# Down-projection weight sums: two by accumulating DMA transfers instead of VectorE adds, and another load order of the quarters

## The chip, the cores and the metric

The kernel runs on one core of a Trainium2 chip. That core has a matrix engine (TensorE, "PE" in the profile, with its weight loads as "PEld"), VectorE (DVE), ScalarE (ACT), GpSimd (POOL) and SyncE (SP). Each engine works through its own queue of instructions in order and waits on semaphores. SP and POOL also issue DMA transfers, which run on 16 shared DMA engines: SP the plain loads from device memory, POOL those that add the source to what is in the destination. The metric is the device time of one launch in microseconds, as the median of several runs; the profile is of one further execution.

## What is computed

A trunk of two layers, run on 512 tokens of one request and 256 of another. Each layer is a half-weighted SwiGLU feed-forward block (FFN), a token mixer, and another FFN, so there are four FFNs (f0 to f3 in the kernel). The change is in the down projection (`w2`) of the FFNs.

```python
def swiglu_ffn(x, w1, w2):
    gate, up = jnp.split(x @ w1, 2, axis=-1)
    return (jax.nn.silu(gate) * up) @ w2

for li in range(DEPTH):
    x = x + 0.5 * swiglu_ffn(rmsnorm(x, norm_g[li, 0]), ffn_w1[li, 0], ffn_w2[li, 0])
    ...
    x = x + mix
    x = x + 0.5 * swiglu_ffn(rmsnorm(x, norm_g[li, 2]), ffn_w1[li, 1], ffn_w2[li, 1])
return rmsnorm(x, final_norm_g)
```

D_MODEL is 1024, D_FF is 2816, all inputs are float32.

## The kernel before

**Precision.** Every float32 weight or activation is split into a high part (a cast on ScalarE) and a low part (a subtraction of the cast from the original on VectorE, for some weights on GpSimd), and each product takes three matmuls: high by high, high by low, low by high.

**Seven products.** The large matrix products are blocked two by two and done with seven block products instead of eight, so sums of weight blocks are needed. For the down projection, a group covers four blocks of 128 rows of `w2`, cut into four quarters of 128 x 1024 numbers: a11, a12 (the left 512 columns, in `srcs` 0 and 1) and a21, a22 (the right 512 columns, in `srcs` 2 and 3). The operands of the seven products are

- p1: a11, p2: a12, p4: a22, as they are loaded;
- p5: a21 + a22, made in place in a21 by a transfer (`into`, L160) that GpSimd issues;
- p7 (`s3`): a21 + a11, made in two half tiles of their own, into which the quarter a21 is loaded once more (L222) and a11 is added by a transfer (L223);
- p6: a11 + (a21 + a22), the "second" sum, made in place in a11;
- p3: a12 + that, the "fourth" sum, made in place in a12.

The second and fourth sums of a down group are VectorE adds (L245), one ahead of p6's split and one ahead of p3's, held in program order (`pin`). The up projection (`w1`) has its own groups of seven, called pairs here, of half the size; they have the same two sums on VectorE, behind the splits of p5 and p4.

**Order of work.** An FFN has five groups. Each is four columns of the up projection (product order p1, p7, p2, p5, p4, p6, p3; matmuls at L669, 384 columns each, 12 to a product) and then one down group. A full group (`DOWN`: p1, p2, p5, p4, p7, p6, p3) has its matmuls at L778, 512 columns each, 18 to a product; after each product's accumulation VectorE adds the PSUM banks into the residual x (L841). An FFN's last group (`LAST`: p1, p2, p6, p7, p4, p5, p3) has 27 matmuls to a product (L811), because two left-over row blocks, the "tail", ride along; the tail has quarters of its own, whose second and fourth sums are already transfers, issued behind the splits of the tail's p1 and p2.

**Staging.** Raw quarters are loaded on SP's queue (L175) into four raw buffers (`wr`, `RAWBUFS`), used in rotation; a down group takes all four, an up pair two. A load waits until the last reader of what its buffer held is done. `stage_next` runs one step of the next group: cast (L238) and subtraction (L239) of one operand into split buffers (`w`, eight of them, `WBUFS`). `ahead` stages as many steps as there are free split buffers, each time PE has finished with a product. So splits run several products ahead of their use. The tail's splits are at L383 and L384. The group after the current one may have its raw loads issued once at most four steps of a down group are left (`inuse`). The instructions' order within each queue is set by a scheduler that goes by its own cost model and by the order of the program; instructions in `pin` keep the program's order.

In an up pair ScalarE copies the result of p1 out of its PSUM bank (L686) and that of p7 (L691), before PE adds p2 and p4 into the same banks; it also does the gates (L694, L709). VectorE's sums of the pair's results are L697 to L710.

Of the kernel before, what the change touches and what calls it, by code (L numbers as in the profile page):

```python
# [58 lines left out]
class Trunk:  # L59
# [102 lines left out]
    def load_next(self):  # L162
        key, srcs, shape, how = self.queue.pop(0)
        if how in (TOK, OUT):
            self.loaded.append((self.tok_steps(key, srcs, how), lambda left: 4 if left > 4 else 0))
            return
        raws = []
        for src in srcs:
            t = self.wp.tile([P, 1024], F32, tag="wr", name=self.name("wr"), bufs=RAWBUFS)
            raw = t[:, : shape[0] * shape[1]].rearrange("p (a b) -> p a b", a=shape[0])  # L170
            if len(srcs) < 4:
                src = src.rearrange("(k p) c -> p k c", p=P)
            step = shape[0] // 2 if key in EARLY else shape[0]
            for lo in range(0, shape[0], step):
                self.last_load = self.nc.sync.dma_start(raw[:, lo : lo + step], src[:, lo : lo + step])  # L175
            raws.append(raw)
        if len(raws) == 1:
            steps = self.plain_steps(key, raws[0], shape)
        else:
            steps = self.quad_steps(key, raws, srcs, how)  # L180
        n, more = len(raws), self.more.get(key)
        if more:
            tail = self.tail_steps(key, more, how)
            steps = [step for both in zip(steps, tail) for step in both]
        if n == 4:
            inuse = lambda left: 4 if left > (8 if more else 4) else 0
        else:
            inuse = lambda left: n
        self.loaded.append((steps, inuse))
# [17 lines left out]
    def quad_steps(self, key, raws, srcs, order):  # L207
        nc = self.nc
        flat = lambda t: t.rearrange("p a b -> p (a b)")
        up = len(raws) == 2  # L210
        if up:
            a11, a12, a21, a22 = (flat(t[:, h : h + 4, :]) for t in raws for h in (0, 4))
            part = lambda i, k: srcs[i].rearrange("(k p) c -> p k c", p=P)[:, k : k + 4, :]
            three = [part(1, 0)] + ([part(0, 4)] if order == OPEN else [])
        else:
            a11, a12, a21, a22 = (flat(t) for t in raws)
            three = [srcs[2][:, i : i + 1, :] for i in range(2)]
        spare = up and (PLAIN[key[0]] == 2 or key[1] > 3)
        s3 = []
        for i, src in enumerate(three):  # L220
            t = self.wp.tile([P, 512], F32, tag="s3", name=self.name("s3"), bufs=2)
            self.last_load = nc.sync.dma_start(t.rearrange("p (a b) -> p a b", a=src.shape[1]), src)  # L222
            self.into(t, a11 if up else a11[:, i * 512 : (i + 1) * 512])  # L223
            s3.append(t)
        self.into(a21, a22)
        if order == OPEN:
            self.into(s3[1], a21)

        def split(name, srcs, eng=None):
            if up:  # L230
                w = self.wtile()
                hi, lo = w[:, :512], w[:, 512:]
            else:
                hi, lo = self.wtile(), self.wtile()
            n = srcs[0].shape[-1]
            for i, src in enumerate(srcs):
                h, l = (t[:, i * n : (i + 1) * n] for t in (hi, lo))
                nc.scalar.copy(h, src)  # L238
                (eng or nc.vector).tensor_sub(l, src, h.bitcast(F32))  # L239
            view = lambda t: t.rearrange("p (a b) -> p a b", a=4 if up else 2)  # L240
            self.staged[(*key, name)] = (view(hi), view(lo), 1 if up else 2)

        own = {"p1": [a11], "p2": [a12], "p3": [a12], "p4": [a22], "p5": [a21], "p6": [a11], "p7": s3}
        pin = self.tc.keep_in_program_order
        add = {"second": lambda: nc.vector.tensor_add(a11, a11, a21), "fourth": lambda: nc.vector.tensor_add(a12, a12, a11)}  # L245
        before = {} if up else {"p6": "second", "p3": "fourth"}
        behind = {"p5": "second", "p4": "fourth"} if up else {}

        if order == OPEN:
            own.update({"p3": s3[1:], "p7": s3[:1]})  # L250
            add = {"second": lambda: self.into(a11, a21)}
            behind, pin = {"p1": "second"}, lambda ins: None

        def step(name):
            if name in before:
                pin(add[before[name]]())
            split(name, own[name], nc.gpsimd if spare and name == "p5" else None)
            if name in behind:
                pin(add[behind[name]]())

        gated = lambda i: order == OPEN and i >= GATED
        return [(1 if up else 2, lambda name=name: step(name), gated(i)) for i, name in enumerate(order)]

    def tail_steps(self, key, srcs, order):
# [368 lines left out]
    def gated(self, pss, act=None, dve=None):  # L633
        t = self.tmp(H)
        with self.tc.issue_after(act) if act else nullcontext():
            self.nc.scalar.activation(t, pss[0], AF.Silu)
        with self.tc.issue_after(dve) if dve else nullcontext():
            self.nc.vector.tensor_mul(t, t, pss[1])
        return t
# [1183 lines left out]
```

## Time and profile before

| what | value |
|---|---|
| median of 3 runs | 2753.04 us (2751.81 to 2754.34) |
| profiled execution, its own time | 2752.44 us |
| its span, first to last instruction | 2750.7 us |
| granted TensorE clock, mean | 0.999 |
| ScalarE waiting for the second or fourth sum on VectorE | 175.9 us in 52 waits, up to 6.1 |
| ScalarE waiting for a transfer into a raw buffer | 66.4 us in 28 waits, up to 5.2 |
| DMA moved | 340.71 MB, 124 GB/s on the mean |
| of it on GpSimd's queue | 97.41 MB, 20.4% of the 16 DMA engines |

How to read the rows. A row of a timeline has the start in us from the span's start, the duration (of several merged instructions from the first start to the last end), engine, source line, operation, output<-input by the program's names, and the count; in brackets the idle time of the engine before it and what ended that. A row of the waits has who waited, for whom, the total in us, how often, and the longest. A group row has the count, the busy time in us and the mean of one in ns, then the idle time before. A row of DMA issues has the count, the size of one and the median time from issue to landing in us. "SPq" is SP's queue of DMA issues; a row of it shows the issue, not the landing.

### The profile page before, as it was taken

The page shows a single profiled execution, that of the slowest core. Times are in us where ns is not written, and L with a number is a line of the kernel's source. Part 1 is how long each engine was busy: PE and PEld are TensorE (multiplying, and loading weights), DVE is VectorE, ACT ScalarE, POOL GpSimd, SP SyncE. Part 2 cuts the span into 40 slices and gives each one's busy share as a digit, 9 for nine tenths or more (in the row PEclk, how much of TensorE's full clock was granted, in tenths as well). Part 3 has the DMA queues.
Part 4 walks back from the last instruction along what each step waited for, and adds up shares of the span by engine and source line. Part 5 has one row for each costly group of instructions (what it writes and reads, how often), then busy time and mean ns, then how long its engine had stood idle before and what let it go on. Part 6 is the DMA issues. An engine that isn't in the chain of part 4 may idle for free.

```text
span 2750.7 us, 41100 instructions
## 1 busy us (share of the span) xinstructions
PE 2732.9 (99%) x15059; PEld 2540.4 (92%) x15059; DVE 2192.8 (80%) x3791; ACT 1408.3 (51%) x2665; POOL 470.4 (17%) x534
## 2 busy tenths in 40 slices
PE   9999999999999999999999999999999999999998
PEld 8999999989999889999998999999888889999997
DVE  8788788767877888788878987887847869788877
ACT  6344444634455675444455643444458855444454
POOL 1111121200000111211121121112005621211120
PEclk9999999999999999999999999999999999999999
DMA  6554556741122755655455555545424435555453
GB/s 178 127 128 116 125 142 165 226 142 39 39 59 65 201 131 124 146 134 127 118 132 141 116 146 130 130 114 141 129 78 111 89 75 121 143 134 131 117 133 111
DMA packets 363259, 340.71 MB, mean 124 GB/s; under 512 B 15320, under 2 KB 275888, under 8 KB 363056
## 3 DMA queue, kind: packets, MB, share of 16 engines
q1 hardware_dynamic: 307200, 227.18, 27.9%
q0 software_dynamic: 51552, 97.41, 20.4%
q10 hardware_dynamic: 4304, 13.49, 1.4%
q8 instruction: 118, 1.93, 0.3%
q14 instruction: 85, 0.70, 0.1%
HBM read 228.45 MB, written 15.73 MB: 89 GB/s over the span
## 4 chain that ended last, share of the span: by engine, by line
PE 80%; DVE 1%; ACT 1%; DMA 0%; issue 0%; POOL 0%; ACTq 0%; POOLq 0%; DVEq 0%
PE ps L669 33%; PE ps L778 12%; PE ps L994 6%; PE ps L811 6%; PE ps L379 5%; PE ps L378 5%; PE ps L380 5%; PE ps L1057 3%; PE ps L1162 1%; PE ps L475 1%; PE ps L1677 1%; PE ps L1138 1%; PE ps L1639 0%; PE ps L1640 0%; PE ps L1689 0%; PE ps L1690 0%
## 5 line engine op out<-in xcount | busy, mean ns | idle before, releaser
L669 PE MATMUL ps<-big,w 128*128 128x384 f32 x6972 | 1213.2, 334 | 0.0
L669 PEld LDWEIGHTS ps<-big,w 128*128 128x128 f32 x6972 | 1209.5, 188 | 1.4
L238 ACT CAST w<-wr 128x512 fp32r<-128x512 f32 (+1 forms) x615 | 429.6, 705 | 664.1 <-PE ps L669 325.1
L239 DVE TENSOR_TENSOR w<-wr,w 128x512 fp32r<-128x512 f32 (+1 forms) x541 | 436.2, 810 | 144.3 <-ACT w L238 116.3
L778 PE MATMUL ps<-w,big 128*128 128x512 f32 x2016 | 461.1, 390 | 1.4 <-DVE x L841 1.4
L778 PEld LDWEIGHTS ps<-w,big 128*128 128x128 f32 x2016 | 376.7, 188 | 81.7 <-ACT big L383 4.0
L160 POOL DMA_DIRECT2D s<-wr x135 | 118.8, 891 | 1235.5 <-DVE wr L245 307.8
L841 DVE SCALAR_TENSOR_TENSOR x<-ps,x 128x512 f32<-128x512 f32 x420 | 273.0, 683 | 11.5 <-PE ps L811 11.2
L384 DVE TENSOR_TENSOR big<-tA,big 128x384 fp32r<-128x384 f32 x308 | 187.7, 620 | 21.4 <-ACT big L383 21.3
L383 ACT CAST big<-tA 128x384 fp32r<-128x384 f32 x308 | 152.6, 514 | 77.5 <-DVE tA L703 31.6
L160 POOL DMA_DIRECT2D wr<-wr x115 | 101.7, 885 | 529.0 <-DVE big L384 122.8
L378 PE MATMUL ps<-big,w 128*128 128x384 f32 x544 | 187.2, 345 | 0.6 <-DVE big L455 0.6
L379 PE MATMUL ps<-big,w 128*128 128x384 f32 x544 | 183.1, 337 | 0.2 <-DVE big L455 0.2
L380 PE MATMUL ps<-big,w 128*128 128x384 f32 x544 | 182.6, 336 | 0.3 <-DVE w L384 0.3
L994 PE MATMUL ps<-w,big 128*128 128x512 f32 x756 | 178.1, 393 | 0.1
L811 PE MATMUL ps<-w,big 128*128 128x512 f32 x756 | 174.4, 391 | 0.5 <-DVE x L841 0.5
L811 PEld LDWEIGHTS ps<-w,big 128*128 128x128 f32 x756 | 141.1, 188 | 30.4 <-DVE x L841 1.5
L994 PEld LDWEIGHTS ps<-w,big 128*128 128x128 f32 x756 | 140.3, 188 | 28.9 <-DVE w L384 0.6
L239 POOL TENSOR_TENSOR w<-wr,w 128x512 fp32r<-128x512 f32 x74 | 106.1, 1433 | 87.1 <-ACT w L238 84.4
L384 DVE TENSOR_TENSOR w<-wr,w 128x1024 fp32r<-128x1024 f32 (+1 forms) x74 | 88.1, 1198 | 30.2 <-ACT w L383 28.9
L245 DVE TENSOR_TENSOR wr<-wr,wr 128x512 f32<-128x512 f32 (+1 forms) x120 | 111.4, 928 | 0.0
L383 ACT CAST w<-wr 128x1024 fp32r<-128x1024 f32 (+1 forms) x74 | 75.7, 1029 | 69.5 <-PE ps L379 35.7
(251 smaller groups left out, 3692.6 us busy)
## 6 DMA issues: line engine op xcount, KB each, us to landing
wr<-in_ffn_w_dram SPq DMA_DIRECT2D x254, 512.0 KB, 4.0
s<-wr POOLq DMA_DIRECT2D x135, 256.0 KB, 4.6
s<-in_ffn_w_dram SPq DMA_DIRECT2D x126, 256.0 KB, 3.2
wr<-wr POOLq DMA_DIRECT2D x86, 256.0 KB, 4.2
wr<-in_hg_w_in_dram SPq DMA_DIRECT2D x32, 512.0 KB, 3.8
wr<-wr POOLq DMA_DIRECT2D x29, 512.0 KB, 4.6
spill<-x ACTq DMA_DIRECT2D x12, 512.0 KB, 3.9
kept<-big POOLq DMA_DIRECT2D x8, 768.0 KB, 6.0
```

Of the source, the lines that this page charges most:

```text
L238: nc.scalar.copy(h, src)
L239: (eng or nc.vector).tensor_sub(l, src, h.bitcast(F32))
L378: nc.tensor.matmul(out, a[0], b[0], start=first, stop=False)
L379: nc.tensor.matmul(out, a[0], b[1], start=False, stop=False)
L380: nc.tensor.matmul(out, a[1], b[0], start=False, stop=last)
L383: self.last_hi = self.nc.scalar.copy(hi, src).ins
L384: self.last_lo = self.nc.vector.tensor_sub(lo, src, hi.bitcast(F32)).ins
L669: self.nc.tensor.matmul(ps, a[x], b[y], start=first and k == 0 and i == 0, stop=k == 3 and i == 2, skip_group_check=True,)
L778: nc.tensor.matmul(ps, a[x], w[y], start=name == chain and kp == 0 and q == 0, stop=kp == 1 and q == 2, skip_group_check=True,)
L811: nc.tensor.matmul(ps, a[x], w[y], start=name == chain and k == 0 and q == 0, stop=k == 2 and q == 2, skip_group_check=True,)
L841: self.nc.vector.scalar_tensor_tensor(x, ps, c, x, ALU.mult, ALU.add)
L994: nc.tensor.matmul(ps, x[:, sl], y, start=fresh and k == 0 and q == 0, stop=k == 3 and q == 2, skip_group_check=True,)
```

## The change

Three edits, all for the down groups (`up` is false there, and only down groups have four `srcs` here).

- The four quarters are loaded in the order a21, a22, a11, a12 instead of a11, a12, a21, a22. The buffers go round in that order too.
- The transfer a21 += a22 stands ahead of the loads and transfers of s3 in the program, instead of behind them.
- The second sum (a11 += a21) and the fourth (a12 += a11) are accumulating transfers of 128 x 1024 numbers that GpSimd issues, behind the splits of p1 and of p2, instead of VectorE adds ahead of the splits of p6 and p3. They aren't pinned.

```diff
-        raws = []
-        for src in srcs:
+        raws = {}
+        for i in (2, 3, 0, 1) if len(srcs) == 4 else range(len(srcs)):
+            src = srcs[i]
...
-            raws.append(raw)
+            raws[i] = raw
+        raws = [raws[i] for i in range(len(srcs))]
...
+        if not up:
+            self.into(a21, a22)
         s3 = []
         for i, src in enumerate(three):
...
             self.into(t, a11 if up else a11[:, i * 512 : (i + 1) * 512])
             s3.append(t)
-        self.into(a21, a22)
+        if up:
+            self.into(a21, a22)
...
         add = {"second": lambda: nc.vector.tensor_add(a11, a11, a21), "fourth": lambda: nc.vector.tensor_add(a12, a12, a11)}
-        before = {} if up else {"p6": "second", "p3": "fourth"}
-        behind = {"p5": "second", "p4": "fourth"} if up else {}
+        behind = {"p5": "second", "p4": "fourth"}
...
+        elif not up:
+            add = {"second": lambda: self.into(a11, a21), "fourth": lambda: self.into(a12, a11)}
+            behind, pin = {"p1": "second", "p2": "fourth"}, lambda ins: None

         def step(name):
-            if name in before:
-                pin(add[before[name]]())
             split(name, own[name], nc.gpsimd if spare and name == "p5" else None)
             if name in behind:
                 pin(add[behind[name]]())
```

`into` is `self.nc.gpsimd.dma_start(out, src, accum_op=ALU.add)`.

## The prediction

> **What bounds the kernel now.** I read the page's head first, then its chain of work, then the waits of the matmul engine, and only then the stages that the change touches.
>
> ```profile
> span 2750.7 us, 41100 instructions
> ...
> PE 2732.9 (99%) x15059; PEld 2540.4 (92%) x15059; DVE 2192.8 (80%) x3791; ACT 1408.3 (51%) x2665; POOL 470.4 (17%) x534
> ...
> PE 80%; DVE 1%; ACT 1%; DMA 0%; issue 0%; POOL 0%; ACTq 0%; POOLq 0%; DVEq 0%
> ```
>
> The matmul engine (PE) is idle for 2750.7 - 2732.9 = 17.8 us of the span, start and end included, and the chain that ends last runs through PE; VectorE (DVE), ScalarE (ACT) and GpSimd (POOL) hold hardly any of it. The change removes no matmul. So whatever it takes off VectorE, the time can fall by at most what PE waits for, and the waits for engines of this kind are few. From the view of PE's waits:
>
> ```profile
> PE ps L778 <- DVE x L841: 1.4, 1, 1.4
> ...
> PE ps L811 <- DVE x L841: 0.5, 1, 0.5
> ```
>
> These two are the only ones of that view that lie in the down products (L778 for a full group, L811 for an FFN's last group). Each is a single event. All other down groups run without a gap, at a pace seen in the chain in order of time:
>
> ```profile
> 1115.62 58.26 PE ps L669 x336
> 1173.88 28.64 PE ps L778 x126
> ```
>
> That is 58.26/336 = 0.173 us a matmul in the up pairs, so 12 x 0.173 = 2.1 us a product, and 28.64/126 = 0.227 us in the down group, so 18 x 0.227 = 4.1 us a product. These two paces set every deadline below.
>
> **The change, part by part.** There are 20 down groups, 16 full ones and 4 last ones, and each has one "second" and one "fourth" sum. The groups by line and shape give their price, and the view of DMA issues gives that of what comes instead:
>
> ```profile
> L245 DVE TENSOR_TENSOR wr<-wr,wr 128x1024 f32<-128x1024 f32 x40 | 48.6, 1215 | 0.0
> wr<-in_ffn_w_dram SPq DMA_DIRECT2D x254, 512.0 KB, 4.0
> wr<-wr POOLq DMA_DIRECT2D x29, 512.0 KB, 4.6
> L160 POOL DMA_DIRECT2D wr<-wr x115 | 101.7, 885 | 529.0 <-DVE big L384 122.8
> ```
>
> *Removed:* 40 adds of 1.215 us, 48.6 us of VectorE. None stood on the chain, and PE was running beside them, so by itself this is worth 0 us. *Added:* 40 accumulating transfers of 512 KB, 0.885 us of issue on GpSimd's queue and about 4.6 us to land. That is 40 x 0.885 = 35 us of an engine that is busy for 17%, again off the chain. What can count is only when weights become ready and which queue stands behind a wait.
>
> *An ordinary group (the one used from 1173.7).* The rows are the loads on SP's queue, and in the second fence ScalarE's casts and copies:
>
> ```profile
> 1140.04 4.47 SPq L175 DMA_DIRECT2D wr<-in_ffn_w_dram  x2
> 1156.53 0.37 SPq L175 DMA_DIRECT2D wr<-in_ffn_w_dram  x1
> 1158.76 0.37 SPq L175 DMA_DIRECT2D wr<-in_ffn_w_dram  x1
> ```
>
> ```profile
> 1159.40 1.05 ACT L238 CAST w<-wr 128x1024 fp32r<-128x1024 f32 x1 [1.46 <-PE ps L669]
> 1160.62 0.53 ACT L709 ACTIVATE tA<-tA 128x384 f32<-128x384 f32 x1 [0.17 <-DVE tA L708]
> 1161.49 0.48 ACT L686 COPY tA<-ps 128x384 f32<-128x384 f32 x1 [0.34 <-PE ps L669]
> ...
> 1163.95 1.05 ACT L238 CAST w<-wr 128x1024 fp32r<-128x1024 f32 x1
> 1168.52 1.05 ACT L238 CAST w<-wr 128x1024 fp32r<-128x1024 f32 x1 [2.45 <-DMA wr<-wr]
> 1177.82 1.14 ACT L238 CAST w<-s 128x512 fp32r<-128x512 f32 x2 [0.25 <-PE ps L778]
> 1187.06 1.05 ACT L238 CAST w<-wr 128x1024 fp32r<-128x1024 f32 x1 [6.09 <-DVE wr L245]
> ```
>
> The four quarters use the four raw buffers in the order in which these come free; the last two wait for the pair before. Today these are a21 and a22, so p5's sum is late and the cast of p5 (1168.52) waits 2.45 us. With the new order a21 and a22 go out at 1140 and 1144, that wait goes, and a11 and a12 take the late places. p1 is the first step cast, so here is the **new wait**: a11 lands at 1156.53 + 4.0 = 1160.5, and the cast of p1 moves from 1159.40 to 1160.5, by 1.1 us. Behind it in ScalarE's queue stand the gate (L709) and the copy out of PSUM (L686): 1160.5 + 1.05 + 0.53 + 0.48 = 1162.6. The pair that runs on PE then began at 1173.7 - 7 x 2.1 = 1159.0; its p2 may not add into p1's bank before that copy, and p1 and p7 fill PE until 1163.2. So 0.6 us are left, and the cost is 0. The weights of p1 are used 14 us later. a12 lands at 1162.8, ahead of its cast at 1163.95: 0.
>
> The sums now ride on GpSimd's queue, one wait after the other: the two halves of s3 read a11 (issued about 1161, landed 1166.5, needed at 1177.82), then a11 += a21 (a new wait, for those landings; landed about 1172), then a12 += a11 (about 1177.5). The cast of p6, at 1187.06 today after 6.09 us behind VectorE's add, can go as soon as a weight buffer is free, some 4 to 5 us sooner; p3 the same. The next instructions behind these waits on GpSimd's queue are transfers for the next pair, and the first subtraction is this:
>
> ```profile
> 1198.01 1.54 POOL L239 TENSOR_TENSOR w<-wr,w 128x512 fp32r<-128x512 f32 x1 [1.27 <-ACT w L238]
> ```
>
> That is 20 us after the last sum has landed: 0. The buffers of a21 and a22 also come free sooner for the next pairs' loads. All of that is earliness that PE doesn't need here: its row shows 126 matmuls without a gap. **Sum for 15 such full groups: 0, bounded below by 0 and above by what the slower case below gives.**
>
> *The first full group of the second FFN (used from 1085.2).* This is the one place where the removed order cost PE something:
>
> ```profile
> 1068.79 0.37 SPq L175 DMA_DIRECT2D wr<-in_ffn_w_dram  x1
> 1072.41 0.37 SPq L175 DMA_DIRECT2D wr<-in_ffn_w_dram  x1
> 1076.79 0.86 POOL L160 DMA_DIRECT2D wr<-wr  x1 [11.86 <-ACT w L238]
> 1082.79 2.00 ACT L238 CAST w<-wr 128x1024 fp32r<-128x1024 f32 x2 [5.24 <-DMA wr<-wr]
> 1083.87 1.23 DVE L239 TENSOR_TENSOR w<-wr,w 128x1024 fp32r<-128x1024 f32 x1 [4.16 <-ACT w L238]
> 1087.47 1.22 DVE L239 TENSOR_TENSOR w<-wr,w 128x1024 fp32r<-128x1024 f32 x1
> 1090.01 0.68 DVE L841 SCALAR_TENSOR_TENSOR x<-ps,x 128x512 f32<-128x512 f32 x1
> 1090.84 24.78 PE L778 MATMUL ps<-w,big 128*128 128x512 f32 x108 [1.36 <-DVE x L841]
> ```
>
> Read from the bottom: PE waits 1.4 us for the first add into x (L841), which stands on VectorE behind two weight subtractions; these wait for ScalarE's cast of p5, and that waits 5.24 us for a21 += a22, whose quarters were asked for at 1068.79 and 1072.41. Loaded in the first two places they are there over 10 us sooner, and the cast of p5 goes when a weight buffer is free. What is late next is a11: 1068.79 + 4.0 = 1072.8 against a cast at 1070.88 today, with the copies behind it as above. I take the whole wait as gone: **-1.4 us** (between 0 and -1.4).
>
> *The last group of the first FFN* has the 0.5 us wait at L811:
>
> ```profile
> 460.32 1.06 ACT L238 CAST w<-wr 128x1024 fp32r<-128x1024 f32 x1 [1.76 <-DVE wr L245]
> 464.91 0.68 DVE L841 SCALAR_TENSOR_TENSOR x<-ps,x 128x512 f32<-128x512 f32 x1
> ```
>
> ScalarE's cast of p6, third in that order, waits for VectorE's second sum; its subtraction and the add into x (464.91) come after it on VectorE. With a transfer instead, VectorE has 1.2 us less to do ahead of that add: **-0.5 us** (between 0 and -0.5). The other three last groups show no such wait.
>
> Sum: -1.9 us. The profiled execution took 2752.44 us, 1.74 more than its span; the median of the three runs is 2753.04, 0.60 above it. So 2752.44 - 1.9 = 2750.5 for the like of the profiled one, and **2751.1 us** against the median.
>
> **The rivals.**
>
> *Nothing that PE feels (0.27).* The two waits are replaced by others of their size: p1 is late by two microseconds in the very group where p5 is no longer. Then 2753.0. For it: both are single events of a schedule that shifts. Against: five microseconds of ScalarE's wait go, at most two come.
>
> *Slower: ScalarE stuck at the first quarter (0.08).* The mechanism is the new wait at p1, in all 20 groups. It decides when a11 lands later than 4.0 + 0.6 = 4.6 us after its issue: then the copy at L686 comes late, and p2 of the pair stands still. As a far bound I take the slowest load of FFN weights on the page:
>
> ```profile
> big<-in_ffn_w_dram SPq DMA_DIRECT2D x20, 256.0 KB, 5.7
> ```
>
> 5.7 - 4.6 = 1.1 us in 20 groups is 22 us: 2775. At a tenth of a microsecond over the point it is 2 us. Against: a21 += a22 will have landed before a11 is asked for, so little runs beside it.
>
> *Slower: the tail's transfers behind the new ones (0.05).* In an FFN's last group p6 is third, and its tail sum goes through the same queue:
>
> ```profile
> 1463.78 0.87 POOL L160 DMA_DIRECT2D big<-big  x1 [4.16 <-DVE tA L703]
> 1463.57 36.99 PE L811 MATMUL ps<-w,big 128*128 128x512 f32 x162
> 1469.62 0.61 ACT L383 CAST w<-big 128x512 fp32r<-128x512 f32 x1
> ```
>
> p1 and p2 take 2 x 27 x 0.227 = 12.3 us, so p6 starts at 1475.8: 6 us behind the tail's cast at 1469.62. With a11 landed at 1450.1, s3 at 1456.2 and the new sums at 1461.5 and 1466.7, the tail's transfer goes out 2 to 4 us later than 1463.78, inside the 6. It decides above 6 us; if both new transfers took 7.5 us there, it would be 1456.9 + 15 = 1472 instead of 1463.78, 8 late, so 2 us in each of 4 groups: 2761. [...]
>
> *Much faster (0.03).* The weight loads on PE's row have gaps of their own:
>
> ```profile
> L778 PEld LDWEIGHTS ps<-w,big 128*128 128x128 f32 x2016 | 376.7, 188 | 81.7 <-ACT big L383 4.0
> ```
>
> If these gaps were waits for weights, earlier weights would give tens of microseconds: up to the 81.7 of this row, 2671. Against: 0.227 us of matmul against 0.188 of load leaves 0.04 x 2016 = 79 us in any case, and only 4.0 has a releaser. [...]
>
> **How the numbers follow.** The chances are 0.57 for the forecast, and for the rivals as given. About 0.2% (5.5 us) is what a measurement of this kernel can tell from no change. Faster than that needs the last rival: 0.03. Slower: nearly all of 0.08 and half of 0.05, so 0.11. The rest, 0.86, is within. The range takes the forecast and the first rival, 2751.1 to 2753.0 (0.84 together), with the 1.3 us by which the three runs lie around their median, another 1.2 below (the few short waits left), and 2.7 above for the point of the first-quarter wait just passed: 2748.6 to 2757.0.
>
> **What would show it.** Right: L245 at 128x1024 gone, wr<-wr at 512 KB up from 29 to 69, the PE waits at L778 and L811 gone, no wait of ScalarE for VectorE at L245 before a 1024-wide cast, and instead about 20 waits of some 1 us for the load. Wrong: PE waiting for ScalarE's copies at L686 or L691 once a group (first-quarter rival), or for the casts of the tail at L811; or PE's idle still near 17.8 us. The prediction falls if the third load in a group no longer leaves with the release of the pair before, since a11's time hangs on that.

## The result and the profile after

The changed kernel takes 2764.43 us (median of 6 runs, 2761.70 to 2765.52) against 2753.03 us (6 runs, 2751.81 to 2754.74): a ratio of 1.0038, 95% interval 1.0025 to 1.0051. It is slower by 11.4 us, 0.4%, where the forecast was 2 us faster and the range ended at 2757.0. The profiled execution took 2764.69 us, its span 2762.9.

From the head of the page after, its chain of work, its groups and its DMA issues:

```profile
span 2762.9 us, 41272 instructions
...
PE 2739.5 (99%) x15059; PEld 2544.2 (92%) x15059; DVE 2158.8 (78%) x3751; ACT 1405.0 (51%) x2665; POOL 505.0 (18%) x574
...
PE 45%; ACT 1%; DVE 1%; DMA 0%; issue 0%; ACTq 0%; POOL 0%; SPq 0%; POOLq 0%
...
L783 PE MATMUL ps<-w,big 128*128 128x512 f32 x2016 | 460.7, 390 | 0.0
...
L816 PE MATMUL ps<-w,big 128*128 128x512 f32 x756 | 180.3, 399 | 9.6 <-DVE x L846 9.6
...
wr<-wr POOLq DMA_DIRECT2D x69, 512.0 KB, 5.6
```

The change does what it says: 40 adds of VectorE are gone (3791 to 3751 instructions), and the transfers of 512 KB went from 29 to 69. The full groups (L783, L778 before) have no idle time left, so the 1.4 us wait is gone. All that was lost stands in the FFNs' last groups (L816, L811 before), 756 matmuls of the 15059: 9.6 us of waiting for VectorE's adds into x, where it was 0.5.

The waits of the matmul engine (PE) give that as five events (total, count, longest):

```profile
PE ps L816 <- DVE x L846: 9.6, 5, 2.7
```

The second FFN's last group shows what such an event looks like. PE's rows of the timeline after:

```profile
1465.46 8.36 PE L816 MATMUL ps<-w,big 128*128 128x512 f32 x36
1476.51 23.67 PE L816 MATMUL ps<-w,big 128*128 128x512 f32 x96 [2.69 <-DVE x L846]
```

36 matmuls are the 27 of p1 and the nine of p2's first row block. p2 accumulates in the three PSUM banks of p1, so before its second row block VectorE must have added p1's second bank into x. PE stands still until then, 2.69 us in the row. The rest of the loss is a slower clock behind the gap. From the view of time windows after, the five microseconds behind the gap of each of the four last groups (columns: window, length, PE busy and matmuls, granted clock, DMA share, GB/s):

```profile
466.50:471.50 5.00, 5.00 (x15) 0.66 0.93 262
1476.50:1481.50 5.00, 4.99 (x15) 0.66 0.87 202
1965.90:1970.90 5.00, 4.99 (x15) 0.66 0.65 156
2720.90:2725.90 5.00, 5.00 (x22) 1.00 0.29 50
```

15 matmuls instead of 22 in three of the four: 7 x 0.227 = 1.6 us each, 4.8 us together. Waits and clock make 9.6 + 4.8 = 14.4 us in the last groups, less the 0.5 of before; the 1.4 us of the full groups come off. That gives +12.5, against a span longer by 12.2 us.

**Why the add is late.** ScalarE's rows (ACT) of that group, first after, then before:

```profile
1458.92 1.03 ACT L243 CAST w<-wr 128x1024 fp32r<-128x1024 f32 x1
1461.54 0.62 ACT L388 CAST w<-big 128x512 fp32r<-128x512 f32 x1 [1.59 <-PE ps L674]
1466.80 1.05 ACT L243 CAST w<-wr 128x1024 fp32r<-128x1024 f32 x1 [4.64 <-DMA wr<-wr]
1467.75 0.51 ACT L388 CAST big<-tA 128x384 fp32r<-128x384 f32 x1
1468.17 0.52 ACT L714 ACTIVATE tA<-tA 128x384 f32<-128x384 f32 x1
1470.08 0.98 ACT L388 CAST big<-tA 128x384 fp32r<-128x384 f32 x2 [1.39 <-DVE tA L715]
```

```profile
1463.80 0.51 ACT L383 CAST big<-tA 128x384 fp32r<-128x384 f32 x1 [3.52 <-DVE tA L703]
1464.35 0.53 ACT L709 ACTIVATE tA<-tA 128x384 f32<-128x384 f32 x1
1465.51 0.98 ACT L383 CAST big<-tA 128x384 fp32r<-128x384 f32 x2 [0.63 <-DVE tA L710]
1468.25 1.06 ACT L238 CAST w<-wr 128x1024 fp32r<-128x1024 f32 x1 [1.76 <-DVE wr L245]
```

The 1024-wide cast with the wait is p6's in both. Before, it stands behind the gate (ACTIVATE) of the last up pair and behind the casts of that pair's results; after, it stands ahead of all of them. There it waits 4.64 us for the second sum's transfer, and the gate, which has nothing to do with that cast, comes only behind it: it starts 1468.17 - 1465.46 = 2.7 us after the group's first matmul, against 1464.35 - 1463.57 = 0.8 before.

VectorE passes it on. Its rows after, then before (TENSOR_TENSOR of 128x1024 at L244 is p6's subtraction, at L245 the second sum):

```profile
1467.88 1.23 DVE L244 TENSOR_TENSOR w<-wr,w 128x1024 fp32r<-128x1024 f32 x1 [1.67 <-ACT w L243]
...
1470.43 0.69 DVE L846 SCALAR_TENSOR_TENSOR x<-ps,x 128x512 f32<-128x512 f32 x1
...
1475.77 0.68 DVE L846 SCALAR_TENSOR_TENSOR x<-ps,x 128x512 f32<-128x512 f32 x1
```

```profile
1465.86 0.68 DVE L841 SCALAR_TENSOR_TENSOR x<-ps,x 128x512 f32<-128x512 f32 x1
...
1466.93 1.22 DVE L245 TENSOR_TENSOR wr<-wr,wr 128x1024 f32<-128x1024 f32 x1
...
1469.47 1.22 DVE L239 TENSOR_TENSOR w<-wr,w 128x1024 fp32r<-128x1024 f32 x1
...
1472.10 0.68 DVE L841 SCALAR_TENSOR_TENSOR x<-ps,x 128x512 f32<-128x512 f32 x1
```

The second add into x starts 1475.77 - 1465.46 = 10.3 us after the group's first matmul, and started 1472.10 - 1463.57 = 8.5 us after it before: 1.8 us later. That doesn't explain 2.69 us yet. 36 matmuls take 8.2 us, and the add of before ended at 8.53 + 0.68 = 9.2; by the same rule PE should have stood still for 1.0 us before as well, and its row has no gap. The answer is in PE's own queue. The order of the matmuls at the start of a last group, by product and row block, with their counts, as the built programs have it:

```
before: p1/0 x9, p1/1 x9, p1/2 x9, p2/0 x9, p6/0 x5, p2/1 x9, p2/2 x9, p6/0 x4, p6/1 x9, ...
after:  p1/0 x9, p1/1 x9, p1/2 x9, p2/0 x9, p2/1 x9, p2/2 x9, p6/0 x9, p6/1 x9, ...
```

Before, the scheduler had put five matmuls of p6 ahead of the one that needs the add. They fill 5 x 0.227 = 1.1 us (the filler, in what follows), so the add was due at 8.2 + 1.1 = 9.3 and ended at 9.2: a tenth of a microsecond of slack, which no wait shows. After, it is due at 8.2 and ends at 11.0: 2.8 us by this sum, 2.69 in the row. The trace bears the order out in the one last group of before where PE does wait, the first FFN's: it stops after 41 matmuls, the 36 and these five.

```profile
455.64 9.50 PE L811 MATMUL ps<-w,big 128*128 128x512 f32 x41
465.65 4.64 PE L811 MATMUL ps<-w,big 128*128 128x512 f32 x19 [0.52 <-DVE x L841]
```

### The profile page after: what moved, and what is told of

Read it like the earlier page. It is cut to its first block, busy times and chain, and to the rows that moved or that the text cites. A ratio compares the mean times of both kernels' runs of the same rounds, so it can differ in the third digit from the quotient of the medians.

```text
span 2762.9 us, 41272 instructions
## 1 busy us (share of the span) xinstructions
PE 2739.5 (99%) x15059; PEld 2544.2 (92%) x15059; DVE 2158.8 (78%) x3751; ACT 1405.0 (51%) x2665; POOL 505.0 (18%) x574
## 5 line engine op out<-in xcount | busy, mean ns | idle before, releaser
L244 DVE TENSOR_TENSOR w<-wr,w 128x512 fp32r<-128x512 f32 (+1 forms) x541 | 440.0, 817 | 149.5 <-ACT w L243 112.3
L783 PE MATMUL ps<-w,big 128*128 128x512 f32 x2016 | 460.7, 390 | 0.0
L783 PEld LDWEIGHTS ps<-w,big 128*128 128x128 f32 x2016 | 376.5, 188 | 80.1 <-ACT big L388 2.4
L160 POOL DMA_DIRECT2D wr<-wr x155 | 136.4, 880 | 846.9 <-DVE w L244 180.6
L389 DVE TENSOR_TENSOR big<-tA,big 128x384 fp32r<-128x384 f32 x308 | 179.9, 595 | 24.0 <-ACT big L388 24.0
L816 PE MATMUL ps<-w,big 128*128 128x512 f32 x756 | 180.3, 399 | 9.6 <-DVE x L846 9.6
L388 ACT CAST big<-tA 128x384 fp32r<-128x384 f32 x308 | 152.6, 514 | 68.8 <-DVE tA L715 32.1
L816 PEld LDWEIGHTS ps<-w,big 128*128 128x128 f32 x756 | 144.4, 192 | 42.0 <-DVE x L846 10.9
L244 POOL TENSOR_TENSOR w<-wr,w 128x512 fp32r<-128x512 f32 x74 | 105.2, 1421 | 116.2 <-ACT w L243 115.5
L388 ACT CAST w<-wr 128x1024 fp32r<-128x1024 f32 (+1 forms) x74 | 75.7, 1029 | 69.8 <-PE ps L384 35.9
L702 DVE TENSOR_TENSOR tA<-tA,ps 128x384 f32<-128x384 f32 x80 | 44.0, 550 | 79.0 <-PE ps L674 78.9
```

Source lines behind the costliest of these rows:

```text
L160: self.nc.gpsimd.dma_start(out, src, accum_op=ALU.add)
L389: self.last_lo = self.nc.vector.tensor_sub(lo, src, hi.bitcast(F32)).ins
L783: nc.tensor.matmul(ps, a[x], w[y], start=name == chain and kp == 0 and q == 0, stop=kp == 1 and q == 2, skip_group_check=True,)
L816: nc.tensor.matmul(ps, a[x], w[y], start=name == chain and k == 0 and q == 0, stop=k == 2 and q == 2, skip_group_check=True,)
```

## The experiments

The first theory was **GpSimd's queue** (A in the expectations): the new transfer of the second sum stands ahead of the tail's transfers and makes them late. Its rivals were a11 and a12 arriving last (B), the bytes of the new transfers (C) and a cost spread over all groups (D). **ScalarE's queue** (F), with p6's cast ahead of the gate because VectorE's pinned sum no longer keeps it back, came up only when e5 had gone against A, and PE's filler only with the last two runs. Times are medians; the kernel before, on the same chips, lay between 2752.63 and 2753.10 us (21 runs in each set).

| kernel | us | runs | ratio to before | PE's wait for the adds into x in the last groups: total us, times, longest |
|---|---|---|---|---|
| e1 full groups only | 2750.26 | 11 | 0.9990 (0.9981 to 0.9999) | 0.7, 1, 0.7 |
| e2 last groups only | 2766.65 | 5 | 1.0049 (1.0035 to 1.0063) | 9.0, 5, 2.9 |
| e4 last groups: sums on VectorE | 2751.17 | 11 | 0.9994 (0.9985 to 1.0003) | 1.3, 2, 0.9 |
| e5 last groups: sums behind the tail's | 2768.63 | 5 | 1.0057 (1.0045 to 1.0070) | 13.2, 7, 3.7 |
| e3 last groups: old load order | 2771.43 | 4 | 1.0067 (1.0054 to 1.0081) | 12.2, 8, 2.2 |
| e10 last groups: only second by transfer | 2762.57 | 5 | 1.0038 (1.0026 to 1.0051) | 8.8, 5, 3.4 |
| e9 last groups: only fourth by transfer | 2751.54 | 11 | 0.9996 (0.9987 to 1.0005) | 1.3, 2, 0.9 |
| e8 p6's cast behind the gate | 2749.14 | 11 | 0.9988 (0.9979 to 0.9997) | none |
| e11 after, with p6's filler | 2756.53 | 11 | 1.0014 (1.0005 to 1.0022) | 5.6, 6, 1.7 |
| e12 e1, without the filler | 2755.22 | 11 | 1.0008 (0.9999 to 1.0018) | 4.2, 4, 1.5 |
| e6 load order alone | 2750.81 | 11 | 0.9993 (0.9984 to 1.0002) | 0.8, 1, 0.8 |
| e7 e1, old load order | 2752.23 | 11 | 0.9998 (0.9989 to 1.0007) | 0.5, 1, 0.5 |

### Which groups: e1, e2, e4

e1 makes all three edits in the 16 full groups only, e2 in the four last groups only, and e4 all edits but the sums of the last groups, which VectorE makes again. The edits are conditions on the order of a group; e1's (e2 has `LAST` for `DOWN`):

```diff
-        for i in (2, 3, 0, 1) if len(srcs) == 4 else range(len(srcs)):
+        for i in (2, 3, 0, 1) if len(srcs) == 4 and how == DOWN else range(len(srcs)):
...
-        if not up:
+        early = not up and order == DOWN
+        if early:
             self.into(a21, a22)
...
-        elif not up:
+        elif not up and order == DOWN:
             add = {"second": lambda: self.into(a11, a21), "fourth": lambda: self.into(a12, a11)}
```

and e4's:

```diff
+        before = {} if up or (order == DOWN) else {"p6": "second", "p3": "fourth"}
...
-        elif not up:
+        elif not up and order == DOWN:
             add = {"second": lambda: self.into(a11, a21), "fourth": lambda: self.into(a12, a11)}
...
         def step(name):
+            if name in before:
+                pin(add[before[name]]())
```

> The change in the 16 full down groups alone; the 4 last groups load and add as before. Theory A (the loss comes from the last groups, where the transfer of the second sum stands ahead of the tail's transfers on GpSimd's queue): 2751.5 us, PE's wait of 1.4 us at the full groups gone, the 0.5 us wait in the first FFN's last group as before. Rivals B (a11 and a12 arriving last in the last groups is what costs) and C (the bytes of two more 512 KB transfers beside the tail's loads): the same 2751.5, since the last groups are as before. Rival D (a cost spread over all groups, such as ScalarE waiting for the first quarter): above 2756.

> The change in the 4 last groups alone; the 16 full groups as before. Theories A, B and C: 2764.4 + 1.4 = 2765.8 us, with about 10 us of PE's waits for the adds into x in the last groups and the 1.4 us wait at the full groups back. Rival D: below 2760, four twentieths of the loss.

> As the changed kernel, but in the last groups the second and fourth sums are VectorE adds again; the load order and the early a21 += a22 stay there. Theory A: 2751.5 us, the tail's transfers back to within 3 us of the group's first matmul and no PE wait above 0.7 us in the last groups. Rival B: 2763 to 2765, since a11 and a12 still arrive last. Rival C: 2751.5.

e1 took 2750.26 us and e2 2766.65: the full groups gain about 2.5 us, and the four last ones lose about 14, so the cost isn't spread over all groups (D). In e2 PE's wait at a full group is back, with 2.0 us. e4, at 2751.17, says that of the last groups' edits it is the sums by transfer that cost; their load order (B) doesn't.

### The transfers as such: e5, e3

e5 puts the last groups' second sum behind the tail's first two transfers on GpSimd's queue, and the fourth behind the tail's others, so that nothing new stands ahead of the tail:

```diff
+        elif order == LAST:
+            own_into = {"p2": (a11, a21), "p6": (a12, a11)}
+            behind = {}
         elif not up:
...
+            if order == LAST and name in own_into:
+                ahead = (self.tail_first, self.tail_into) if name == "p2" else (self.tail_second,) * 2
+                with self.tc.issue_after(ahead[0].ins), self.tc.issue_after(ahead[1].ins):
+                    self.into(*own_into[name])
```

> As the changed kernel with all its transfers, but in the last groups the second sum goes behind the tail's first two transfers on GpSimd's queue (issued after p2's split), and the fourth behind the tail's other two (after p6's split). Theory A: 2751 us, PE waits in the last groups below 1 us in all. Rival B: 2763 to 2765. Rival C (the bytes): 2759 or more, since the same bytes move at the same time.

2768.63 us, slower still: theory A had 2751, B had less, and only C's "2759 or more" allows it. ScalarE's rows of the second FFN's last group in e5, which began at 1465.38 (the last row is the tail's cast for p6):

```profile
1469.78 1.05 ACT L243 CAST w<-wr 128x1024 fp32r<-128x1024 f32 x1 [7.68 <-DMA wr<-wr]
1470.73 0.51 ACT L395 CAST big<-tA 128x384 fp32r<-128x384 f32 x1
1471.15 0.52 ACT L721 ACTIVATE tA<-tA 128x384 f32<-128x384 f32 x1
...
1475.48 0.61 ACT L395 CAST w<-big 128x512 fp32r<-128x512 f32 x1
```

The tail's sum was there in time, its cast waited for nothing. But the second sum came 3 us later, p6's cast waited 7.68 us instead of 4.64, and the gate behind it went with it. The rival that I had priced, the tail behind the new transfers, fell here.

e3 leaves the last groups' quarters in the old load order, with a21 += a22 behind s3, and keeps the sums as transfers:

```diff
-        for i in (2, 3, 0, 1) if len(srcs) == 4 else range(len(srcs)):
+        for i in (2, 3, 0, 1) if len(srcs) == 4 and how == DOWN else range(len(srcs)):
...
-        if not up:
+        early = not up and order == DOWN
+        if early:
             self.into(a21, a22)
...
-        if up:
+        if not early:
             self.into(a21, a22)
```

> As the changed kernel, but in the last groups the quarters come in the old order, a11 and a12 first, and a21 += a22 behind s3; both sums stay transfers. Rival B (a11 arriving late, so that s3 and all behind it is late): 2751 to 2753 us. Theory F: still slow, 2760 or more, since now a21 += a22 is late and the second sum waits for it.

2771.43 us. With the second sum still later, p6's cast waits longer, again ahead of the gate. From ScalarE's timeline of the same group in e3:

```profile
1468.63 1.05 ACT L244 CAST w<-wr 128x1024 fp32r<-128x1024 f32 x1 [5.81 <-DMA wr<-wr]
```

So the load order of the last groups helps there; it isn't the cause.

### Which sum: e10, e9

e10 makes only the last groups' second sum by a transfer, e9 only the fourth; the other one is VectorE's, pinned as before:

```diff
+        elif order == LAST:
+            add["second"] = lambda: self.into(a11, a21)
+            before, behind = {"p3": "fourth"}, {"p1": "second"}
```

```diff
+        elif order == LAST:
+            add["fourth"] = lambda: self.into(a12, a11)
+            before, behind = {"p6": "second"}, {"p6": "fourth"}
```

> As the changed kernel, but in the last groups the fourth sum is a VectorE add again; the second stays a transfer. Theory F and rival A: 2762 to 2765 us, since p6 waits for the second. Rival C (the bytes): half the loss, 2757.

> As the changed kernel, but in the last groups the second sum is a VectorE add again (pinned in program order ahead of p6's split) and the fourth a transfer behind p6's split. Theory F and rival A: 2751 us. Rival C (the bytes): 2757.

e10 has most of the loss (2762.57, which is 12.3 of the 14.2 us between e1 and the changed kernel), e9 hardly any of it (2751.54). It is the second sum, the one that p6's cast needs. The bytes of the transfers (C) aren't the cause: by them each of the two would have shown half. The filler goes with the second sum as well: in the first FFN's last group PE stops after 41 matmuls in e9 and after 36 in e10. In one group, the second FFN's, e10 also shows that an earlier landing doesn't put the gate back in its place. From ScalarE's timeline there, where the group's first matmul ran at 1466.70:

```profile
1466.95 1.05 ACT L243 CAST w<-wr 128x1024 fp32r<-128x1024 f32 x1 [3.55 <-PE ps L682]
1467.90 0.51 ACT L396 CAST big<-tA 128x384 fp32r<-128x384 f32 x1
1468.31 0.52 ACT L722 ACTIVATE tA<-tA 128x384 f32<-128x384 f32 x1
```

Here what ended the wait is PE: with eight split buffers, p6's cast needs the one that the last up product frees. The sum had landed. The gate is still late (1.6 us after the group's start instead of 0.8), and PE's wait in this group is 2.00 us instead of 2.69. In the other three groups of e10 the cast still waits for the transfer (4.35, 2.96 and 4.37 us, the 11.7 us in three waits of ScalarE's view).

### The place in ScalarE's queue: e8

e8 is the changed kernel with one thing more: in the last groups p6's cast and subtraction are staged, and issued, behind the last cast and subtraction of the up pair's results.

```diff
-                nc.scalar.copy(h, src)
-                (eng or nc.vector).tensor_sub(l, src, h.bitcast(F32))
+                late = order == LAST and name == "p6"
+                with self.tc.issue_after(self.mixed[0]) if late else nullcontext():
+                    nc.scalar.copy(h, src)
+                with self.tc.issue_after(self.mixed[1]) if late else nullcontext():
+                    (eng or nc.vector).tensor_sub(l, src, h.bitcast(F32))
...
-            if self.held + n > WBUFS or (gated and self.shut):
+            if self.held + n > WBUFS or (gated and self.shut) or (self.wait and len(self.loaded[0][0]) == 10):
                 return
...
         tail, ts = {}, {}
+        self.wait = True
...
         self.mix(*(ts[i] for i in range(4)), put_tail, True)
+        self.wait = False
+        self.mixed = self.last_hi, self.last_lo
```

> As the changed kernel with all its loads and transfers and the same order on GpSimd's queue; only ScalarE's cast of p6 in the last groups (and its subtraction on VectorE) is put behind the casts of the last pair's results (the mix), as VectorE's add had kept it before. Theory F (the cast of p6, which waits for the second sum's transfer, stands on ScalarE ahead of the last pair's gate and the casts of its results, and holds up VectorE and the adds into x behind them): 2751 to 2752 us, PE waits at the last groups below 1.5 us in all. Rival A (the tail's transfers, late on GpSimd's queue): 2762 or more, since that queue is as in the changed kernel. Both at once: in between, 2755 to 2759.

2749.14 us: all of the loss is gone, with every sum still a transfer. ScalarE's rows of that group in e8, then PE's and VectorE's second add into x:

```profile
1461.77 0.53 ACT L717 ACTIVATE tA<-tA 128x384 f32<-128x384 f32 x1
...
1465.34 1.05 ACT L245 CAST w<-wr 128x1024 fp32r<-128x1024 f32 x1
...
1469.96 0.62 ACT L391 CAST w<-big 128x512 fp32r<-128x512 f32 x1 [2.65 <-DMA big<-big]
```

```profile
1460.98 36.93 PE L819 MATMUL ps<-w,big 128*128 128x512 f32 x162
```

```profile
1466.68 0.68 DVE L849 SCALAR_TENSOR_TENSOR x<-ps,x 128x512 f32<-128x512 f32 x1
```

The gate is back at 0.8 us after the start, p6's cast waits for nothing, and 162 matmuls run without a gap. The second add starts 5.7 us after the group's start, where before it was 8.5: VectorE has neither the second sum (1.22) nor p6's subtraction (1.22) ahead of it. That relief is what the change was able to give here. e8 moves the cast on ScalarE and the subtraction on VectorE together, and what is staged behind them with them; their shares were not separated. The tail's cast for p6 comes 9.0 us after the start, as late as in the changed kernel (L388 in after, 1474.23 - 1465.46 = 8.8), and costs nothing. e8 is the fastest version, 0.12% below before (0.03% to 0.21%); from e1 it can't be told apart.

### PE's filler: e11, e12

e8's matmuls stand in the program's order, without the filler, and don't need it. For the changed kernel the two runs ask what the filler is worth. e11 puts five matmuls of p6's first row block between p2's first and second; e12 is e1 (last groups as before, sums on VectorE) with p6's first matmul held behind p2's last. In both, ScalarE's and VectorE's orders up to there are unchanged.

```diff
+                if (name, i) == ("p2", 1):
+                    wh6, wl6 = self.take((*key, "p6"))
...
+                    for m in range(0, 5):
+                        (a, w), (x, y) = early[m // 3], ((0, 0), (0, 1), (1, 0))[m % 3]
+                        with self.tc.issue_after(mm.ins):
+                            mm = nc.tensor.matmul(banks[("p6", 0)], a[x], w[y], start=m == 0, stop=False, skip_group_check=True)
```

```diff
+                        with self.tc.issue_after(mm.ins) if (name, i, k, q) == ("p6", 0, 0, 0) else nullcontext():
+                            mm = nc.tensor.matmul(
```

> After, with five matmuls of p6's first bank put between p2's first and second bank on the matmul engine's queue of the last groups, as the kernel before has them; ScalarE's and VectorE's orders up to there are as in after. If the lost filler is part of the cost: five matmuls are 5 x 0.227 = 1.1 us, so the waits for the adds into x fall from 2.0 to 2.8 us a group to 0.9 to 1.7, about 2760 us; about 2755 if the slow matmuls behind the waits go as well. If only ScalarE's queue counts: waits as long as in after and about 2764 us.

> The kernel with the change in the full groups only, and in the last groups p6's first matmul held behind p2's last, as in after; VectorE's sums and ScalarE's order as before. If the lost filler is part of the cost: the second add into x ends 9.2 us after the group's start and the matmul engine gets there after 8.2, so about 1.0 us a group, 4 us together, about 2754.5 us. If only ScalarE's queue counts: no new wait, 2750.3 us.

e11 took 2756.53 us, 7.9 less than the changed kernel; e12 took 2755.22, 5.0 more than e1. PE's rows of that group in e11 (L822 is the filler), then in e12:

```profile
1463.32 8.36 PE L828 MATMUL ps<-w,big 128*128 128x512 f32 x36
1471.52 1.29 PE L822 MATMUL ps<-w,big 128*128 128x512 f32 x5
1474.27 25.91 PE L828 MATMUL ps<-w,big 128*128 128x512 f32 x113 [1.46 <-DVE x L858]
```

```profile
1464.95 8.36 PE L821 MATMUL ps<-w,big 128*128 128x512 f32 x36
1474.22 26.14 PE L821 MATMUL ps<-w,big 128*128 128x512 f32 x114 [0.91 <-DVE x L851]
```

In e11 the wait is 1.46 instead of 2.69, by the 1.1 us of the filler, although the add is as late as in the changed kernel (10.2 us after the start). Over the four groups the waits fall from 9.6 to 5.6 us, and the slow clock behind them is gone, 4.8 us more: 8.8 by the rows, 7.9 by the medians. In e12 a wait of 0.9 us comes up in three of the four groups, as the sum above says (9.2 - 8.2 = 1.0), and 1.5 in the first FFN's. So either half alone costs 5 to 6 us, measured from e1 (e12 +5.0, e11 +6.3), and both together 14.2; the 2.9 us over the sum are less than the 4.8 of the clock, which neither half alone brings on (behind e12's four waits a matmul takes 0.229 to 0.230 us; behind e11's longest the granted clock is 1.00, as quoted in the last section).

### The full groups' gain: e6, e7

e6 keeps the load order and the early a21 += a22 in all groups, with all sums on VectorE; e7 is e1 with the old load order, so only the full groups' sums are transfers.

```diff
-        behind = {"p5": "second", "p4": "fourth"}
+        before = {} if up or (False) else {"p6": "second", "p3": "fourth"}
+        behind = {"p5": "second", "p4": "fourth"} if up else {}
...
-        elif not up:
+        elif not up and False:
             add = {"second": lambda: self.into(a11, a21), "fourth": lambda: self.into(a12, a11)}
             behind, pin = {"p1": "second", "p2": "fourth"}, lambda ins: None
...
+            if name in before:
+                pin(add[before[name]]())
```

```diff
-        for i in (2, 3, 0, 1) if len(srcs) == 4 else range(len(srcs)):
+        for i in (2, 3, 0, 1) if len(srcs) == 4 and False else range(len(srcs)):
...
-        if not up:
+        early = not up and False
+        if early:
             self.into(a21, a22)
...
-        if up:
+        if not early:
             self.into(a21, a22)
...
-        elif not up:
+        elif not up and order == DOWN:
```

> All groups load a21 and a22 first and add them early, as in after, but VectorE makes all sums again and no accumulating transfer is added. Order theory (the 2.5 us gained in the full groups come from p1's quarters being there early, so that p1's cast no longer holds up ScalarE): about 2751 us, and the 1.4 us wait of PE at the first full group of the second FFN is gone. Transfer theory (they come from VectorE's relief): about 2753 us, and that wait is still listed.

> Full groups: second and fourth sum by transfers as in after, but the old order of loads, with a21 + a22 added behind s3; last groups as before the change. Order theory: about 2753 us, a wait of PE of 1.4 to 2 us at a full group is listed. Transfer theory: about 2750.5 us and no such wait.

e6 took 2750.81 us and has no wait in a full group; e7 took 2752.23 and has the old one, from its view of PE's waits:

```profile
PE ps L787 <- DVE x L850: 1.1, 1, 1.1
```

The wait goes with the load order (and the early a21 += a22, which no run tells from it), not with VectorE's relief. The times point the same way, but their intervals overlap, so of the 2.5 us of e1 the trace shows 1.4, and where the rest comes from, if it is there, stays open.

## Why the prediction was wrong

**The ceiling** (nothing can gain more than PE's idle 17.8 us) held: the best version gains about 3.5.

**An ordinary full group, 0:** right. In the changed kernel the group like the one quoted is used from 1175.7. PE's row and ScalarE's rows of it:

```profile
1175.69 28.77 PE L783 MATMUL ps<-w,big 128*128 128x512 f32 x126
```

```profile
1161.79 1.05 ACT L243 CAST w<-wr 128x1024 fp32r<-128x1024 f32 x1 [1.88 <-DMA wr<-in_ffn_w_dram]
1162.75 0.52 ACT L714 ACTIVATE tA<-tA 128x384 f32<-128x384 f32 x1
1163.46 0.48 ACT L691 COPY tA<-ps 128x384 f32<-128x384 f32 x1 [0.19 <-PE ps L674]
...
1186.37 1.05 ACT L243 CAST w<-wr 128x1024 fp32r<-128x1024 f32 x1 [3.41 <-PE ps L783]
1187.95 1.06 ACT L243 CAST w<-wr 128x1024 fp32r<-128x1024 f32 x1 [0.53 <-PE ps L783]
```

The new wait of p1's cast for its load is there, the copy behind it still waits for PE and not for the cast, and the casts of p6 and p3 (the last two rows) wait for a buffer from PE instead of a sum. Two sizes were off without costing PE anything: over the whole kernel there are 19 waits of ScalarE for such loads, as forecast in number, but 35.6 us in all, so 1.9 us on the mean and not 1; and p6's cast goes 1186.37 - 1175.69 = 10.7 us after the group's first matmul, and went 1187.06 - 1173.72 = 13.3 us after it before, so it is some 2.7 us sooner and not 4 to 5. ScalarE stuck at the first quarter, the rival with 0.08, did not happen.

**The first full group of the second FFN, -1.4:** right in place, size and reason (e6, e7).

**The last group of the first FFN, -0.5:** here the prediction failed, and with it for all four last groups. It read: "ScalarE's cast of p6, third in that order, waits for VectorE's second sum ... With a transfer instead, VectorE has 1.2 us less to do ahead of that add". The step took the order of ScalarE's queue as given. But it was the pinned sum, with its late place on VectorE, that had kept the cast behind the gate; with the sum unpinned and on another queue, the cast was put ahead of the gate, and what was removed from VectorE came back as a wait of everything behind it on ScalarE. That the cast's place goes with the second sum is shown by e9 and e10; whether the pin alone or the place on VectorE alone keeps it was not tried. What should have been -0.5 us became a wait of 2.55 us in that group and of 1.8 to 2.7 in the others, with 1.6 us of slower clock behind the gap in three of the four.

**The same step again, for the other three groups:** "The other three last groups show no such wait" was taken for room. They had 0.1 us of it, and only with five matmuls of p6 put in between; these moved as well. The prediction used the use of weights on PE as the only due time in a last group (p6's at 12.3 us, 6 us of slack for the tail's cast). The add into x was due at 9.3 and ended at 9.2.

**The rival of the tail's transfers** put 7.5 us on each new transfer in a last group, which no run shows: in the changed kernel the eight of them landed in 4.6 to 6.0 us. It named the place and, with its 2761 us, nearly the size, but the nearness is chance, since the mechanism is another: in e5 the tail's transfers go first and it gets worse, in e8 the tail's cast is as late as in the changed kernel and it costs nothing.

## What to carry to other kernels

When an instruction is taken off an engine's queue, ask what its place had been holding back: an instruction that waited for it is now free to be put earlier in its own queue, and if its new input comes later than that, what stands behind it can wait too, as the gate did here behind p6's cast and its 4.64 us. Keep such an instruction where it was with an explicit order, as e8 does, and compare the order of instructions on every queue, the matmuls' too, before trusting a sum of removed work. An engine without a visible wait is not an engine with slack: work out when each input was due and when it came.

## What the runs showed of the hardware that was not expected

Short gaps of PE were followed by a lower clock. Behind the waits of 2.55, 2.69 and 1.79 us in the changed kernel the granted clock was 0.66 on the mean of the next 5 us (15 matmuls where 22 fit), and behind 2.17 us in its last FFN it was 1.00 (the windows at the top). In e11 the longest waits are 1.46 and 1.67 us, and the same view shows nothing of it there:

```profile
1474.20:1479.20 5.00, 4.93 (x22) 1.00 0.92 218
2713.60:2718.60 5.00, 5.00 (x22) 1.00 0.30 51
```

Length alone doesn't decide, since 2.17 us was spared and 1.79 us was not. In e10's second FFN a wait of 2.00 us was spared too: the 101 matmuls behind it took 23.19 us, 0.230 each, where the 96 behind the 2.69 us of the changed kernel took 23.67, 0.247 each. What decides was not tried. In the changed kernel a wait of 1.79 to 2.69 us cost up to 1.6 us more than itself (7 x 0.227, the matmuls missing from the five microseconds behind it).
